# A decode step of a hybrid RG-LRU and mLSTM layer: decode products in pieces of four tokens, and a unit's half products in another order

## The chip, the cores and the metric

The kernel runs on one core of a Trainium2 chip. The metric is the device time of one execution in microseconds, the median of several runs. TensorE (PE) multiplies, VectorE (DVE), ScalarE (ACT) and GpSimd (POOL) work on tiles in SBUF, SyncE (SP) issues loads. POOL issues most stores. Matmul results stand in banks of PSUM.

## The reference

One layer reads 1024 new prompt positions and one new position each for eight running sequences (decode), with one combined input projection to 7168 columns and some gates:

```python
hn = rmsnorm(x, g_norm)
u = hn @ w_in                       # x: 1024 wide; columns xa, za, q, k, v, o, zb, gates
yA, hA, bufA = rglru_branch(xa, ...)
h, C, n, m = mlstm_seq(q, k, v, ig, lf, C0, n0, m0)
yB = sigmoid(uo) * h ; yB = yB * rsqrt(mean(yB * yB) + EPS) * g_mhead
x = x + concat([yA * silu(za), yB * silu(zb)]) @ w_out
```

For a decode token and each of four heads the matrix memory C (256 x 256) is replaced, and its product with the query is wanted:

```python
C_new = carry_scale * C + decay * k[:, None] * v[None, :]
num   = P @ v + ginter * (q @ C)
```

All values are float32. Outputs are the projected prompt and decode rows and all new states, C of every sequence and head among them.

## The kernel before, in words

**Units.** The input projection's weights are cut into blocks of 256 columns, and two of them form one of 14 units (`UNITS`, L44), unit 0 in a start stage, units 1 to 13 in the main loop at the end of the program text shown. A unit holds its raw weights in two tiles, raw0 and raw1, for the lower and upper half of the 1024 input rows; each has two parts, one for each column block. Its product with the prompt is done with seven block products in place of eight: P1, P2, P5, P6, P7, P3, P4 in this order, each in two halves s = 0 and 1. P1, P6, P7 and P4 add into banks X (tag `kv`, one for each half), P2, P5 and P3 into banks Y (tag `o`).

**Splitting.** Each factor is split in a high and a low part, and one logical matmul is three (`mm3`, L66 to L68: high by high, high by low, low by high). A half product is 12 matmuls of 512 columns, or 24 of 256 in units of v and o. `prep` (L276) makes the weights' two parts: ACT casts the high part (L72), DVE subtracts for the low part (L73), into two of six `ws` slots. It runs two products ahead. Before some of them DVE adds or subtracts blocks of raw weights in place (L279 to L288). When P7 or P4 is prepared, the next unit's raw0 or raw1 is loaded whole (L243, two loads of 512 KB on SP's queue).

**Decode rows.** At the preparation of P5, before the raw weights are changed in place, `dec_unit` (L251) multiplies the eight decode rows by the unit's 512 columns: 32 float32 matmuls in four column tiles of 32 (L257), 64 records in the trace.

**Decode states.** When q, k and v of a head are complete, `decode_steps` puts nine steps in a queue: one to set up, and eight tokens. A token's C (two blocks of 128 x 256) is scaled by ACT (L988), gets its outer product from DVE in two instructions (L990), and is stored by POOL. C has four buffers and the broadcast v two. After each second token `products` multiplies the two new states by their queries (L1009): four float32 matmuls in four column tiles, eight records, into bank `qp`.

**What sets the order.** After each half product `pop_bg` takes steps from queues of other work; a token step is taken at every second half, from unit 10 on at every third (`DEC`, L46). `late` holds what follows one or two halves later. When the queues are empty and all heads are complete, `m_start` begins the prompt's matrix part. A scheduler then sets the final order of instructions on each engine by its own estimates, and adds the waits.

Of the kernel before, what the change touches and what calls it, by code (L numbers as in the profile page):

```python
# [9 lines left out]
F32 = mybir.dt.float32  # L10
# [7 lines left out]
P = 128  # L18
# [33 lines left out]
def hymba_kernel(  # L52
# [181 lines left out]
    def load_raw(u, b, parts=(0, 1)):  # L234

        if u >= len(units):
            return
        if (u, b) not in raws:
            raws[u, b] = rawp.tile([P, 4, 512], F32, tag=f"raw{b}", name=f"raw{b}_{u}")
        for a in parts:  # L240
            kind, j = units[u][a]
            c = COL[kind] + j * 256
            ld(raws[u, b][:, :, a * 256:(a + 1) * 256],  # L243
               w_in[0, b * HT:(b + 1) * HT, c:c + 256].rearrange("(k p) c -> p k c", p=P))
# [3 lines left out]
               "z": lambda j: dz[:, 2 * j:2 * j + 2], "x": lambda j: dxz[:, 0, 2 * j:2 * j + 2],  # L248
               "y": lambda j: dxz[:, 1, 2 * j:2 * j + 2]}

    def dec_unit(u):  # L251

        pz = ps("tr" if u < 2 else "o", [P, 512])[:, 0:P]
        for k in range(KC):
            for g in range(4):
                w = blk(u, g // 2, k // 4)[:, k % 4, (g % 2) * P:(g % 2 + 1) * P]
                TE.matmul(pz[32 * g:32 * g + 32, :], hnd[:, NB * k:NB * k + 32], w, start=k == 0, stop=k == KC - 1,  # L257
                          skip_group_check=True)
# [12 lines left out]
    wops = {}  # L271

    def blk(u, a, b):
        return raws[u, b][:, :, a * 256:(a + 1) * 256]

    def prep(u, q):  # L276
        if q == Q_P5:
            dec_unit(u)
            V.tensor_tensor(blk(u, 0, 0), blk(u, 0, 0), blk(u, 1, 0), op=ALU.subtract)  # L279
            V.tensor_tensor(blk(u, 1, 0), blk(u, 1, 0), blk(u, 1, 1), op=ALU.add)  # L280
        if q == Q_P6:
            V.tensor_tensor(blk(u, 1, 0), blk(u, 1, 1), blk(u, 0, 0), op=ALU.subtract)
        src = {Q_P1: (0, 0), Q_P2: (0, 1), Q_P5: (1, 0), Q_P6: (1, 0), Q_P7: (0, 0), Q_P3: (0, 1), Q_P4: (1, 1)}
        hi, lo = ws([P, 4, 256], f"wh{u}_{q}"), ws([P, 4, 256], f"wl{u}_{q}")
        split(hi, lo, blk(u, *src[q]))
        wops[u, q] = hi, lo
        if q == Q_P6:
            V.tensor_tensor(blk(u, 0, 1), blk(u, 0, 1), blk(u, 1, 0), op=ALU.subtract)  # L288
        b = {Q_P7: 0, Q_P4: 1}.get(q)
        if b is not None:  # L290
            if u + 1 < len(units):
                load_raw(u + 1, b)
            else:
                if b == 1:
                    r_open(0)

    px = {}

    def product(u, q):

        kind = units[u][0][0]
        wh, wl = wops.pop((u, q))
        bh, bl = cb[q]
        first, last = q in (Q_P1, Q_P2, Q_P5), q in (Q_P2, Q_P3, Q_P4)
        for s in range(2):
            if q == Q_P1:
                px["X", s] = ps("kv", [P, 512])
            if q in (Q_P2, Q_P5):
                px["Y", s] = ps("o", [P, 512])
            X, Y = px["X", s], px.get(("Y", s))  # L310
            out = X if q in (Q_P1, Q_P6, Q_P7, Q_P4) else Y
            if kind in "vo":
                for i in range(2):
                    t = slice((2 * s + i) * P, (2 * s + i + 1) * P)
                    for k in range(4):
                        mm3(out[:, i * 256:(i + 1) * 256], bh[:, k, t], bl[:, k, t], wh[:, k, :], wl[:, k, :],
                            first and i == 0 and k == 0, last and i == 1 and k == 3)
            else:
                c = slice(s * P, (s + 1) * P)
                for k in range(4):  # L320
                    mm3(out, wh[:, k, c], wl[:, k, c], bh[:, k, :], bl[:, k, :], first and k == 0, last and k == 3)
            evac(u, q, s, X, Y)
            yield

    def evac(u, q, s, X, Y):
        if q == Q_P1:
            px["s1", s] = t = sg([P, 512], "s1")
            A.copy(t, X)
        elif q == Q_P2:
            t = px.pop(("s1", s))  # L330
            V.tensor_tensor(t, t, Y, op=ALU.add)
            emit_out(u, 0, 0, s, t)
        elif q == Q_P5:
            px["s5", s] = t = sg([P, 512], "s5")
            A.copy(t, Y)
# [609 lines left out]

    def dec_open():
        p2 = fpr["p"]
        fetch_C(0)
        fetch_C(1)

        fpr["qsel"] = qsel = p2.tile([P, 2, 36], F32, tag="qsel", name="qsel")
        G.memset(qsel, 0.0)
# [16 lines left out]
    def decode_steps(h):  # L969
# [5 lines left out]
        def first():  # L975
# [5 lines left out]
            fetch_v(h, 0)  # L981

        def token(b):
            i = h * NB + b

            def f():
                vb_, C = ds_.pop(("v", i)), ds_["C", i]
                A.mul(C, C, dGI[:, b, h:h + 1])  # L988
                for kb in range(2):
                    V.scalar_tensor_tensor(C[:, kb, :], vb_, st["kw"][:, kb, b:b + 1], C[:, kb, :],  # L990
                                           op0=ALU.mult, op1=ALU.add)
                stq(s_C[0, b, h].rearrange("(kb p) v -> p kb v", p=P), C)
                if b + 1 < NB:
                    fetch_v(h, b + 1)
                if b % 2:
                    late.append(lambda: late.append(products))
                else:
                    fetch_C(i + 2)
                    fetch_C(i + 3)


            def products():
                if b == 1:
                    st["pq"] = ps("qp", [P, 512])
                pq = st["pq"]
                for g in range(4):
                    bb, kb = b - 1 + g // 2, g % 2
                    q, n = (qfirst[:, kb, bb, :], 32) if b == 1 else (qsel[:, kb, 4 * bb:4 * bb + 4], 4)
                    TE.matmul(pq[32 * g:32 * g + n, 0:256], q, ds_["C", h * NB + bb][:, kb, :], start=b == 1,  # L1009
                              stop=b == NB - 1, skip_group_check=True)  # L1010
                for bb in (b - 1, b):
# [12 lines left out]
        return [first] + [token(b) for b in range(NB)]  # L1024


    def bh(t):
# [645 lines left out]

    gg = gates()
    bg.extend([lambda: next(gg, None)] * 17 + [rd_open])
    last_u = len(units) - 1
    unit_of = {p: u for u, pair in enumerate(units) for p in pair}
    done_h = [max(unit_of[k, h] for k in "qkv") for h in range(NH)]

    def m_start():  # L1680
        state["m"] = True
        bg.append(m_open1)
        for n in range(NH):
            bg.extend(m_first(n))

    preps(LEAD)
    part = 0
    for n, (u, q) in enumerate(seq):
        preps(n + 1 + LEAD)
        for _ in product(u, q):  # L1690
            pop_bg(2 if u == 1 or u == last_u else 1, 1, part % DEC[1 if u >= DEC[0] else 2] == 1)
            part += 1
        if u == last_u:
            wo_due(q)
        if q == 6:
            for kind, j in units[u]:
                if kind == "x":
                    rg_unit(j)
            for half in range(2):
                if u == max(unit_of["v", 2 * half], unit_of["v", 2 * half + 1], 1):  # L1700
                    bg.append(lambda half=half: dec_rows(half))
            for h in range(NH):
                if done_h[h] == u:
                    bg.append(lambda h=h: dcq.extend(decode_steps(h)))
            if u == last_u - 1:
                dgen = decode_outputs()

                def step():
                    next(dgen, None)
                    run_late()  # L1710
                state["out"] = [step] * 5 + [m_open2]
        if not state["m"] and u > max(done_h) and not (bg or rgq or dcq or late):
            m_start()
        if u == last_u and q == 0:
            if not state["m"]:
                while bg or rgq or dcq or late:
                    pop_bg()
                m_start()
            bg.extend(state["out"])
    while bg or late:  # L1720
        pop_bg()
    with tc.issue_after(lastt[0].ins):
# [102 lines left out]
```

## Time and profile before

| | |
|---|---|
| median of 3 runs | 915.67 us (915.23 to 915.72) |
| profiled execution | 913.23 us |
| its span, first to last instruction | 911.3 us |
| PE busy | 899.6 us, 99% |
| DVE, ACT, POOL busy | 739.3, 585.0, 194.2 us |
| mean granted TensorE clock | 0.999 |
| DMA packets | 167.76 MB, mean 184 GB/s |
| split of weights, ACT cast L72 and DVE L73 | 91 each, 1049 ns and 1221 ns |

A row of the timeline has the start in us, the duration in us, the engine, the line, the operation, the target and sources by tile name, the form, and the count; in brackets the idle time before it and what ended it. Matmuls are pipelined, so the durations of neighbours overlap: what one costs is the time from its start to the next start. A float32 matmul leaves two records. A row of the waits has the total, the count and the longest.

### The profile page before, as it was taken

Reading aid. Unit: us, or ns where it says so; the run is one execution under the profiler, and the core shown is the slowest. Engines: PE = TensorE matmul, PEld = TensorE weight load, DVE = VectorE, ACT = ScalarE, POOL = GpSimd, SP = SyncE. Lnnn points to the kernel's source line nnn. Section 1 sums busy time; section 2 is a strip of 40 time slices with the busy share of each in tenths; the row PEclk is TensorE's granted clock in tenths of the full one; section 3 lists DMA queues with packets and bytes.
Section 4 is the critical chain, followed back from the end, with each engine's and each line's share of the span. In section 5 each row is a group of like instructions: output and inputs, shape, how many; then the busy total and the mean of one; then the engine's idle time right before and its main releaser. Section 6 shows DMA issues by size and latency. Waiting matters only on the chain. (4 is left out here: it accounts for less than half of the span.)

```text
span 911.3 us, 16738 instructions
## 1 busy us (share of the span) xinstructions
PE 899.6 (99%) x5889; PEld 762.3 (84%) x5889; DVE 739.3 (81%) x1528; ACT 585.0 (64%) x1086; POOL 194.2 (21%) x322
## 2 busy tenths in 40 slices
PE   8999999999999999999999999999999999999996
PEld 6997778877788997887789999887788888888886
DVE  6974778979698978789889876679998879888973
ACT  7653446867567776576658775446786568566642
POOL 1111112122222232324332334010111111121120
PEclk9999999999999999999999999999999999999999
DMA  6412447465746566548665747345679888855531
GB/s 200 149 64 92 139 147 250 135 205 187 236 128 221 171 203 204 197 145 266 201 237 184 253 139 244 108 133 191 215 234 259 202 216 296 217 142 180 181 124 67
DMA packets 130493, 167.76 MB, mean 184 GB/s; under 512 B 17596, under 2 KB 98564, under 8 KB 130402
## 3 DMA queue, kind: packets, MB, share of 16 engines
q1 hardware_dynamic: 108790, 103.68, 37.4%
q0 software_dynamic: 21616, 63.02, 20.9%
q8 instruction: 46, 0.75, 0.3%
q14 instruction: 37, 0.30, 0.1%
q10 hardware_dynamic: 4, 0.00, 0.0%
HBM read 108.00 MB, written 62.92 MB: 188 GB/s over the span
## 5 line engine op out<-in xcount | busy, mean ns | idle before, releaser
L72 ACT CAST wh<-raw 128x1024 fp32r<-128x1024 f32 x91 | 95.4, 1049 | 79.5 <-DVE raw L280 21.0
L73 DVE TENSOR_TENSOR wl<-raw,wh 128x1024 fp32r<-128x1024 f32 x91 | 111.1, 1221 | 29.4 <-ACT wh L72 15.8
L66 PE MATMUL ps_kv<-cb_hi,wh 128*128 128x512 f32 x320 | 127.4, 398 | 0.0
L68 PE MATMUL ps_kv<-cb_hi,wl 128*128 128x512 f32 x320 | 125.5, 392 | 0.0
L67 PE MATMUL ps_kv<-cb_lo,wh 128*128 128x512 f32 x320 | 125.2, 391 | 0.0
L66 PE MATMUL ps_o<-cb_hi,wh 128*128 128x512 f32 x240 | 95.2, 397 | 0.0
L68 PE MATMUL ps_o<-cb_hi,wl 128*128 128x512 f32 x240 | 93.7, 391 | 0.0
L67 PE MATMUL ps_o<-cb_lo,wh 128*128 128x512 f32 x240 | 93.6, 390 | 0.0
L66 PEld LDWEIGHTS ps_kv<-cb_hi,wh 128*128 128x128 f32 x320 | 60.1, 188 | 15.9 <-issue 3.1
L68 PEld LDWEIGHTS ps_kv<-cb_hi,wl 128*128 128x128 f32 x320 | 60.1, 188 | 13.4 <-issue 0.6
L67 PEld LDWEIGHTS ps_kv<-cb_lo,wh 128*128 128x128 f32 x320 | 60.1, 188 | 12.7 <-issue 0.8
L66 PE MATMUL ps_kv<-wh,cb_hi 128*128 128x256 f32 x192 | 55.1, 287 | 0.0
L67 PE MATMUL ps_kv<-wl,cb_hi 128*128 128x256 f32 x192 | 54.4, 283 | 0.0
L68 PE MATMUL ps_kv<-wh,cb_lo 128*128 128x256 f32 x192 | 54.3, 283 | 0.0
L66 PEld LDWEIGHTS ps_o<-cb_hi,wh 128*128 128x128 f32 x240 | 45.1, 188 | 10.4 <-issue 0.8
L68 PEld LDWEIGHTS ps_o<-cb_hi,wl 128*128 128x128 f32 x240 | 45.0, 188 | 9.9
L66 PE MATMUL ps_o<-wo,mh 128*128 128x512 f32 (+1 forms) x136 | 53.0, 390 | 0.0
L67 PEld LDWEIGHTS ps_o<-cb_lo,wh 128*128 128x128 f32 x240 | 45.1, 188 | 8.9
L68 PE MATMUL ps_o<-wo,ml 128*128 128x512 f32 (+1 forms) x136 | 51.6, 380 | 0.0
L67 PE MATMUL ps_o<-wo,mh 128*128 128x512 f32 (+1 forms) x136 | 51.5, 379 | 0.0
L66 PE MATMUL ps_o<-wh,cb_hi 128*128 128x256 f32 x144 | 41.0, 284 | 0.0
L67 PE MATMUL ps_o<-wl,cb_hi 128*128 128x256 f32 x144 | 40.7, 283 | 0.0
(559 smaller groups left out, 2603.8 us busy)
## 6 DMA issues: line engine op xcount, KB each, us to landing
raw<-in_w_in_dram SPq DMA_DIRECT2D x55, 512.0 KB
Cb<-in_state_mlstm_C_dram SPq DMA_DIRECT2D x32, 256.0 KB
out_dram<-Cb POOLq DMA_DIRECT2D x32, 256.0 KB, 4.9
qk<-d_qk SPq DMA_DIRECT2D x32, 256.0 KB
ring<-d_ro SPq DMA_DIRECT2D x26, 256.0 KB
d_qk<-s POOLq DMA_DIRECT2D x24, 256.0 KB, 4.8
d_x<-s POOLq DMA_DIRECT2D x16, 256.0 KB, 2.8
zsr<-d_y SPq DMA_DIRECT2D x16, 256.0 KB
```

The lines of the kernel that those rows point to most:

```text
L66: TE.matmul(out, ah, bh, start=first, stop=False, skip_group_check=True)
L67: TE.matmul(out, ah, bl, start=False, stop=False, skip_group_check=True)
L68: TE.matmul(out, al, bh, start=False, stop=last, skip_group_check=True)
L72: a = A.copy(hi, src)
L73: V.tensor_tensor(lo, src, hi.bitcast(F32), op=ALU.subtract)
```

## The change

**Decode products.** They are now done for four tokens at a time: eight pieces of eight matmuls (16 records) in place of 16 of four. A piece is put in the queue `full`, and `dec_unit` takes it directly behind its own matmuls. C is fetched four tokens at a time after the products of the four before. The scale by ACT is done one token ahead, and v is fetched two ahead. Tokens are taken at halves 3, 5, 7, 9 and 11 of a unit's 14.

**Half products.** A unit now runs P2s0 P2s1 P1s0 P1s1 P5s0 P5s1 P6s0 P6s1 P3s0 P7s0 P7s1 P3s1 P4s0 P4s1 (the last unit begins with P1). P2's result is copied and P1's added to it, where before P1's was copied. Weights are prepared at halves 0, 2, 4, 6, 8, 11 and 12.

**Raw weights.** raw0 and raw1 are one tile each for all units, and the next unit's weights are loaded by parts as a block is done with: raw0's second part after P6 is prepared, its first after P7, raw1's first after P3, its second after P4. `m_start` is tested after each second half, and its first steps stand some 40 instructions of PE later in unit 12.

```diff
-DEC = 10, 2, 3
+DEC = 3, 5, 7, 9, 11
...
         if (u, b) not in raws:
-            raws[u, b] = rawp.tile([P, 4, 512], F32, tag=f"raw{b}", name=f"raw{b}_{u}")
+            raws[u, b] = raws[0, b] if (0, b) in raws else rawp.tile([P, 4, 512], F32, tag=f"raw{b}", name=f"raw{b}")
...
+        if full:
+            full.popleft()()
         Z = sg([P, P], "Z")
         A.copy(Z, pz)
...
+    FREED = {Q_P6: (0, (1,)), Q_P7: (0, (0,)), Q_P3: (1, (0,)), Q_P4: (1, (1,))}
...
-        b = {Q_P7: 0, Q_P4: 1}.get(q)
-        if b is not None:
-            if u + 1 < len(units):
-                load_raw(u + 1, b)
-            else:
-                if b == 1:
-                    r_open(0)
+        if u + 1 < len(units):
+            if q in FREED:
+                load_raw(u + 1, *FREED[q])
+        elif q == Q_P4:
+            r_open(0)
...
+        if q in (Q_P1, Q_P2):
+            Z = X if q == Q_P1 else Y
+            if ("s1", s) not in px:
+                px["s1", s] = t = sg([P, 512], "s1")
+                A.copy(t, Z)
             else:
+                t = px.pop(("s1", s))
+                V.tensor_tensor(t, t, Z, op=ALU.add)
+                emit_out(u, 0, 0, s, t)
...
+        def ready(b):
+            fetch_v(h, b)
+            fetch_v(h, b + 1)
+            scale(b)
...
-                A.mul(C, C, dGI[:, b, h:h + 1])
+                if b % 4 < 3:
+                    scale(b + 1)
...
-                if b % 2:
-                    late.append(lambda: late.append(products))
-                else:
-                    fetch_C(i + 2)
-                    fetch_C(i + 3)
+                if b % 4 < 2:
+                    late.append(lambda: fetch_v(h, b + 2))
+                if b % 4 == 3:
+                    full.append(products)
...
+                for b0 in (b - 3, b - 1):
+                    for g in range(4):
+                        bb, kb = b0 + g // 2, g % 2
+                        q, n = (qfirst[:, kb, bb, :], 32) if b0 == 0 else (qsel[:, kb, 4 * bb:4 * bb + 4], 4)
+                        TE.matmul(pq[32 * g:32 * g + n, 0:256], q, ds_["C", h * NB + bb][:, kb, :], start=b0 == 0,
+                                  stop=b0 == NB - 2, skip_group_check=True)
...
+                for n in (1, 3):
+                    late.append(lambda n=n: late.append(lambda: [fetch_C(i + n), fetch_C(i + n + 1)]))
...
+        return [first, *steps[:4], lambda: ready(4), *steps[4:]]
...
-    seq = [(u, q) for u in range(1, len(units)) for q in range(7)]
+    last_u = len(units) - 1
+    FIRST = lambda u: (Q_P1, Q_P2) if u == last_u else (Q_P2, Q_P1)
+    seq = [(u, q) for u in range(1, len(units)) for q in (*FIRST(u), *range(2, 7))]
...
+    REST = [(Q_P5, 0), (Q_P5, 1), (Q_P6, 0), (Q_P6, 1), (Q_P3, 0), (Q_P7, 0), (Q_P7, 1), (Q_P3, 1), (Q_P4, 0), (Q_P4, 1)]
+    PREP = 0, 2, 4, 6, 8, 11, 12
...
+    for u in range(1, len(units)):
+        for n, (q, s) in enumerate([(q, s) for q in FIRST(u) for s in range(2)] + REST):
+            if n in PREP:
+                preps(7 * (u - 1) + PREP.index(n) + 1 + LEAD)
+            product(u, q, s)
+            pop_bg(2 if u == 1 or u == last_u else 1, 1, part % 14 in DEC)
```

In the orders below, names end in a running number; `wh4_3` and `wl4_3` are the high and low weights of unit 4's product number 3 (numbers 0 to 6 are P1, P2, P5, P6, P7, P3, P4), `cb_hi` and `cb_lo` the prompt's parts, `hnd` the decode rows, `Cb` a token's C.

PE before, a decode product between the two halves of P6 in unit 4 (L1009):

```order
L67 MATMUL ps_kv_2341<-cb_lo3_194,wh4_3_2400 128x512
L68 MATMUL ps_kv_2341<-cb_hi3_193,wl4_3_2401 128x512
L1009 MATMUL ps_qp_2160<-Cb_2197,qsel_1416 4x256 x2
L1009 MATMUL ps_qp_2160<-Cb_2199,qsel_1416 4x256 x2
L66 MATMUL ps_kv_2367<-cb_hi3_193,wh4_3_2400 128x512
L67 MATMUL ps_kv_2367<-cb_lo3_194,wh4_3_2400 128x512
```

PE now, the decode rows of unit 5 and the second piece of the first head behind them (L1019 is the new line of the products, L259 that of the decode rows):

```order
L259 MATMUL ps_o_2697<-raw0_0_219,hnd_112 32x128 x16
L259 MATMUL ps_o_2697<-raw1_232,hnd_112 32x128 x16
L1019 MATMUL ps_qp_2314<-Cb_2368,qsel_1413 4x256 x2
L1019 MATMUL ps_qp_2314<-Cb_2370,qsel_1413 4x256 x2
L1019 MATMUL ps_qp_2314<-Cb_2372,qsel_1413 4x256 x2
L1019 MATMUL ps_qp_2314<-Cb_2374,qsel_1413 4x256 x2
L66 MATMUL ps_o_2748<-cb_hi1_189,wh5_1_2620 128x512
```

Sixteen groups by themselves became eight groups of twice the size, with decode rows ahead of them.

PE before, from the start stage's end into unit 1 (`ps_tr` takes the decode rows of units 0 and 1, raw1_0 is unit 0's tile, raw0_1 and raw1_1 are unit 1's):

```order
L577 MATMUL ps_o_1017<-wg_213,hnd_112 32x8 x8
L257 MATMUL ps_tr_1029<-raw1_0_232,hnd_112 32x128 x8
L66 MATMUL ps_kv_1123<-cb_hi0_187,wh1_0_1074 128x512
L67 MATMUL ps_kv_1123<-cb_lo0_188,wh1_0_1074 128x512
L257 MATMUL ps_tr_1082<-raw0_1_1064,hnd_112 32x128 x16
L68 MATMUL ps_kv_1123<-cb_hi0_187,wl1_0_1075 128x512
```

PE now, the same place:

```order
L580 MATMUL ps_o_1017<-wg_213,hnd_112 32x8 x8
L259 MATMUL ps_tr_1029<-raw1_232,hnd_112 32x128 x14
L259 MATMUL ps_tr_1080<-raw0_0_219,hnd_112 32x128 x16
L259 MATMUL ps_tr_1080<-raw1_232,hnd_112 32x128 x2
L66 MATMUL ps_o_1121<-cb_hi1_189,wh1_1_1072 128x512
L67 MATMUL ps_o_1121<-cb_lo1_190,wh1_1_1072 128x512
L66 MATMUL ps_o_1174<-cb_hi1_189,wh1_1_1072 128x512
L259 MATMUL ps_tr_1080<-raw1_232,hnd_112 32x128 x14
L68 MATMUL ps_o_1121<-cb_hi1_189,wl1_1_1073 128x512
```

P1's matmuls (wh1_0) stood behind unit 0's decode rows; now P2's (wh1_1) stand there, behind two matmuls on unit 1's raw1, and the six matmuls of unit 0's decode rows that stood in two places of the start stage have come to its end.

PE before, P6 and P7 in unit 1 (L616 transposes parameters):

```order
L67 MATMUL ps_kv_1176<-cb_lo3_194,wh1_3_1230 128x512
L68 MATMUL ps_kv_1176<-cb_hi3_193,wl1_3_1231 128x512
L616 MATMUL ps_s_1166<-idF_78,par_1146 128x49 x8
L66 MATMUL ps_kv_1123<-cb_hi4_195,wh1_4_1275 128x512
L67 MATMUL ps_kv_1123<-cb_lo4_196,wh1_4_1275 128x512
```

PE now:

```order
L67 MATMUL ps_kv_1259<-cb_lo3_194,wh1_3_1228 128x512
L619 MATMUL ps_s_1164<-idF_78,par_1144 128x49 x8
L68 MATMUL ps_kv_1259<-cb_hi3_193,wl1_3_1229 128x512
L66 MATMUL ps_o_1279<-cb_hi5_197,wh1_5_1332 128x512
L67 MATMUL ps_o_1279<-cb_lo5_198,wh1_5_1332 128x512
L66 MATMUL ps_kv_1234<-cb_hi4_195,wh1_4_1274 128x512
L67 MATMUL ps_kv_1234<-cb_lo4_196,wh1_4_1274 128x512
L68 MATMUL ps_o_1279<-cb_hi5_197,wl1_5_1333 128x512
```

P3 (wh1_5) follows P6 (wh1_3) at once, with two matmuls of P7 (wh1_4) ahead of the first use of P3's low part.

More of the change, by code (lines that the diff above doesn't have):

```diff
@@ L249, in hymba_kernel @@
                "y": lambda j: dxz[:, 1, 2 * j:2 * j + 2]}
+    full = deque()
     def dec_unit(u):
@@ L301, in product @@
         kind = units[u][0][0]
-        wh, wl = wops.pop((u, q))
+        wh, wl = wops.pop((u, q)) if s == 1 else wops[u, q]
         bh, bl = cb[q]
         first, last = q in (Q_P1, Q_P2, Q_P5), q in (Q_P2, Q_P3, Q_P4)
[L305 to L317, printed above, removed]
-            else:
[L319 to L332, printed above, removed]
+        if q == Q_P1:
+            px["X", s] = ps("kv", [P, 512])
+        if q in (Q_P2, Q_P5):
+            px["Y", s] = ps("o", [P, 512])
+        X, Y = px.get(("X", s)), px.get(("Y", s))
+        out = X if q in (Q_P1, Q_P6, Q_P7, Q_P4) else Y
@@ new lines, in product @@
+        if kind in "vo":
+            for i in range(2):
+                t = slice((2 * s + i) * P, (2 * s + i + 1) * P)
+                for k in range(4):
+                    mm3(out[:, i * 256:(i + 1) * 256], bh[:, k, t], bl[:, k, t], wh[:, k, :], wl[:, k, :],
+                        first and i == 0 and k == 0, last and i == 1 and k == 3)
+        else:
+            c = slice(s * P, (s + 1) * P)
+            for k in range(4):
+                mm3(out, wh[:, k, c], wl[:, k, c], bh[:, k, :], bl[:, k, :], first and k == 0, last and k == 3)
@@ L947, in dec_open @@
         p2 = fpr["p"]
-        fetch_C(0)
-        fetch_C(1)
+        for i in range(4):
+            fetch_C(i)
         fpr["qsel"] = qsel = p2.tile([P, 2, 36], F32, tag="qsel", name="qsel")
@@ L980, in first, with scale @@
             V.tensor_copy(qfirst[:, :, :, 0], dq[:, 2 * h:2 * h + 2, 0:2])
-            fetch_v(h, 0)
+            ready(0)
+        def scale(b):
+            C = ds_["C", h * NB + b]
+            A.mul(C, C, dGI[:, b, h:h + 1])
+        def ready(b):
+            fetch_v(h, b)
+            fetch_v(h, b + 1)
+            scale(b)
         def token(b):
@@ L992, in f @@
                 stq(s_C[0, b, h].rearrange("(kb p) v -> p kb v", p=P), C)
-                if b + 1 < NB:
-                    fetch_v(h, b + 1)
-                if b % 2:
-                    late.append(lambda: late.append(products))
-                else:
-                    fetch_C(i + 2)
-                    fetch_C(i + 3)
+                if b % 4 < 2:
+                    late.append(lambda: fetch_v(h, b + 2))
+                if b % 4 == 3:
+                    full.append(products)
             def products():
-                if b == 1:
+                if b == 3:
                     st["pq"] = ps("qp", [P, 512])
                 pq = st["pq"]
[L1006 to L1011, printed above, removed]
+                for b0 in (b - 3, b - 1):
[4 more added lines that the diff above has]
+                                  stop=b0 == NB - 2, skip_group_check=True)
+                for bb in range(b - 3, b + 1):
                     del ds_["C", h * NB + bb]
+                for n in (1, 3):
+                    late.append(lambda n=n: late.append(lambda: [fetch_C(i + n), fetch_C(i + n + 1)]))
                 if b == NB - 1:
@@ L1023, in token @@
             return f
-        return [first] + [token(b) for b in range(NB)]
+        steps = [token(b) for b in range(NB)]
+        return [first, *steps[:4], lambda: ready(4), *steps[4:]]
     def bh(t):
@@ L1675, in hymba_kernel @@
     bg.extend([lambda: next(gg, None)] * 17 + [rd_open])
-    last_u = len(units) - 1
     unit_of = {p: u for u, pair in enumerate(units) for p in pair}
@@ L1684, in m_start @@
             bg.extend(m_first(n))
+    REST = [(Q_P5, 0), (Q_P5, 1), (Q_P6, 0), (Q_P6, 1), (Q_P3, 0), (Q_P7, 0), (Q_P7, 1), (Q_P3, 1), (Q_P4, 0), (Q_P4, 1)]
+    PREP = 0, 2, 4, 6, 8, 11, 12
+    DUE = 1, 3, 5, 7, 10, 12, 13
     preps(LEAD)
     part = 0
[L1688 to L1691, printed above, removed]
-            part += 1
[L1693 to L1717, printed above, removed]
-                m_start()
-            bg.extend(state["out"])
@@ new lines, in hymba_kernel, with step @@
+    for u in range(1, len(units)):
[4 more added lines that the diff above has]
+            pop_bg(2 if u == 1 or u == last_u else 1, 1, part % 14 in DEC)
+            part += 1
+            if u == last_u and n in DUE:
+                wo_due(DUE.index(n))
+            if n == 13:
+                for kind, j in units[u]:
+                    if kind == "x":
+                        rg_unit(j)
+                for half in range(2):
+                    if u == max(unit_of["v", 2 * half], unit_of["v", 2 * half + 1], 1):
+                        bg.append(lambda half=half: dec_rows(half))
+                for h in range(NH):
+                    if done_h[h] == u:
+                        bg.append(lambda h=h: dcq.extend(decode_steps(h)))
+                if u == last_u - 1:
+                    dgen = decode_outputs()
+                    def step():
+                        next(dgen, None)
+                        run_late()
+                    state["out"] = [step] * 5 + [m_open2]
+            if n % 2 and not state["m"] and u > max(done_h) and not (bg or rgq or dcq or late):
+                m_start()
+            if u == last_u and n == 1:
+                if not state["m"]:
+                    while bg or rgq or dcq or late:
+                        pop_bg()
+                    m_start()
+                bg.extend(state["out"])
```

4 lines of the change are left out of this document (3 added, 1 removed).

## The prediction

> **What bounds the kernel now.** I read the page's head, then the view of TensorE's waits, then the timeline.
>
> ```profile
> span 911.3 us, 16738 instructions
> PE 899.6 (99%) x5889; PEld 762.3 (84%) x5889; DVE 739.3 (81%) x1528; ACT 585.0 (64%) x1086; POOL 194.2 (21%) x322
> PE ps_tr L531 <- POOL ones L116: 1.1, 1, 1.1
> PE ps_o L67 <- DVE w1l L73: 0.9, 1, 0.9
> PE ps_tr L257 <- DMA raw<-in_w_in_dram: 0.3, 1, 0.3
> ```
>
> TensorE (PE) is busy 899.6 of 911.3 us. The longest single wait is 1.1 us, and no listed wait of a unit's product is for a PSUM bank. So another order of half products can free nothing that the profile shows: I put the spacing of banks at zero. What can change is the time that PE spends in matmuls that do little, and new idle time. The profiled execution took 913.2 us, 2.4 under the median of 915.67; I work on it and carry the difference over.
>
> **Decode products: 16 groups become 8, each behind a unit's decode rows.** The group records at L1009 and one group among 512-column matmuls:
>
> ```profile
> L1009 PE MATMUL ps_qp<-Cb,qsel x96: 379/379/380, 207.6 to 536.4; 128*4 128x256 f32 x96
> L1009 PE MATMUL ps_qp<-Cb,qfirst x32: 379/391/403, 187.3 to 496.1; 128*32 128x256 f32 x32
> 187.01 0.39 PE L68 MATMUL ps_kv<-cb_hi,wl 128*128 128x512 f32 x1
> 187.33 0.64 PE L1009 MATMUL ps_qp<-Cb,qfirst 128*32 128x256 f32 x8
> 188.24 0.39 PE L67 MATMUL ps_kv<-cb_lo,wh 128*128 128x512 f32 x1
> 207.24 0.39 PE L68 MATMUL ps_kv<-cb_hi,wl 128*128 128x512 f32 x1
> 207.56 0.61 PE L1009 MATMUL ps_qp<-Cb,qsel 128*4 128x256 f32 x8
> 208.10 0.50 PE L66 MATMUL ps_kv<-cb_hi,wh 128*128 128x512 f32 x1
> 208.44 0.39 PE L67 MATMUL ps_kv<-cb_lo,wh 128*128 128x512 f32 x1
> 208.67 0.40 PE L68 MATMUL ps_kv<-cb_hi,wl 128*128 128x512 f32 x1
> ```
>
> 128 records in eights are 16 groups. Full-width matmuls start 0.23 us apart (208.44 to 208.67). From 207.24 to 208.44 are 1.20 us, where two steps would take 0.46: the group costs 0.74. At 187 it is 1.23 - 0.46 = 0.77. Four of the one and twelve of the other are 12.0 us. Of this the step from the last full matmul to the group (0.32 for 0.23), and the first full step behind it (0.34 for 0.23), are paid for coming and going, 0.20 a group; the group's own 0.54 holds two rounds of four column tiles.
>
> Now each of eight pieces has four rounds and comes directly behind the 64 records of a unit's decode rows, which pay for coming and going already. How much is a round?
>
> ```profile
> 73.12 1.08 PE L257 MATMUL ps_tr<-raw,hnd 128*32 128x128 f32 x32
> 74.13 0.50 PE L68 MATMUL ps_kv<-cb_hi,wl 128*128 128x512 f32 x1
> 159.12 1.95 PE L257 MATMUL ps_o<-raw,hnd 128*32 128x128 f32 x64
> 161.00 0.50 PE L66 MATMUL ps_kv<-cb_hi,wh 128*128 128x512 f32 x1
> ```
>
> Decode rows: 1.01 us for 32 records and 1.88 for 64, so 0.109 per round of four records and 1.01 - 8 x 0.109 = 0.14 for draining. If a product group drains for as long, its round is (0.54 - 0.14) / 2 = 0.20, and four are 0.80; with the qfirst piece, 0.57 long, 0.83. I take 0.82, so 8 x 0.82 = 6.5. The bounds: were all of a group's 0.54 rounds, a piece costs 1.08 and the saving is 12.0 - 8.6 = 3.4; were coming and going hidden in it as at 0.23 us, a round is 0.155 and the saving 12.0 - 5.0 = 7.0. **Saving 5.5 us.** C is fetched right after a piece, four tokens at a time, and a piece waits on PE only if one of its four states is late; the next unit's decode rows come 14 halves of 12 matmuls at 0.23 us later, 39 us, for eight tokens at the most, so I price that at 0 and keep 0 to 2 us.
>
> By the Trainium skill, "TensorEngine Tiling (Array Packing)", Key Properties, a change of the tiling mode drains TensorE, a change of the tile alone does not. The rows above agree: a group pays for coming and going, a round inside it does not. If the step from the decode rows to the products counted as a change of mode too, each piece would pay one more drain, 0.14 by the row above, and the saving would be 4.4.
>
> **Unit 1 begins with P2, whose weights are not there.** P2 reads block raw1, P1 reads raw0. Unit 1's raw1 can be loaded only when the decode rows of unit 0 have read the old raw1.
>
> ```profile
> 59.24 0.42 PE L257 MATMUL ps_tr<-raw,hnd 128*32 128x128 f32 x6
> 59.59 0.39 PE L66 MATMUL ps_o<-wph,cb_hi 128*128 128x264 f32 x1
> 59.81 0.28 PE L67 MATMUL ps_o<-wpl,cb_hi 128*128 128x264 f32 x1
> 72.45 0.50 PE L66 MATMUL ps_kv<-cb_hi,wh 128*128 128x512 f32 x1
> 72.68 0.98 SPq L243 DMA_DIRECT2D raw<-in_w_in_dram  x2
> 76.74 1.05 ACT L72 CAST wh<-raw 128x1024 fp32r<-128x1024 f32 x1 [3.86 <-DMA raw<-in_w_in_dram]
> 76.76 0.41 PE L257 MATMUL ps_tr<-raw,hnd 128*32 128x128 f32 x4 [0.29 <-DMA raw<-in_w_in_dram]
> 77.82 1.23 DVE L73 TENSOR_TENSOR wl<-raw,wh 128x1024 fp32r<-128x1024 f32 x1 [2.07 <-ACT wh L72]
> 81.64 0.39 PE L66 MATMUL ps_o<-cb_hi,wh 128*128 128x512 f32 x1
> ```
>
> Before, PE goes on with P1 (ps_kv from 72.45) while raw1 travels from 72.68 to 76.74, and P2 starts at 81.64. In the changed order nothing of P1 stands ahead of P2. Reckoned forward: two detours of six records in the start stage (59.24, and one like it) are gone; each cost 0.35, 0.09 coming and 0.10 going, 0.54; their 12 records, three rounds or 0.33, go to the end of unit 0's decode rows. These end at 72.45 - 1.08 + 0.33 = 71.7. The load is issued 0.23 later, 71.9, and lands 4.06 later, 76.0. PE meanwhile has 32 records of unit 1's decode rows on raw0, 1.0 us, and idles from 72.7 to 76.0. Then four records, and idle again until the cast of P2's high half, 1.05, at 77.05. Three full matmuls (0.69) and the other 28 records (seven rounds and the drain, 0.9, and 0.2 coming and going) end at 78.85; the low half is there by 77.1 + 1.23 = 78.4. The remaining 21 matmuls of P2 at 0.23 and two transposes among them (0.1 each, as a round) end at 83.9. There the second product starts; before it was 81.64. **Loss 2.2 us**, the detours' gain in it. The two halves of raw1 are issued together and share the queues; P2 needs one. If it came in half of the 4.06, the loss would be 0.2; if the transfer took a quarter longer, 3.2. What waits there behind ACT's cast is only P1's cast, with 6 us to spare.
>
> **P3 follows P6 at once.** P3's low half needs a ws slot, freed when P5 is done; before, two products (P6, P7) lay between, now one.
>
> ```profile
> 92.31 0.39 PE L68 MATMUL ps_o<-cb_hi,wl 128*128 128x512 f32 x1
> 93.22 1.05 ACT L72 CAST wh<-raw 128x1024 fp32r<-128x1024 f32 x1
> 98.00 1.22 DVE L73 TENSOR_TENSOR wl<-raw,wh 128x1024 fp32r<-128x1024 f32 x1 [4.20 <-PE ps_kv L67]
> 311.82 0.28 PE L68 MATMUL ps_o<-wh,cb_lo 128*128 128x256 f32 x1
> 315.86 1.22 DVE L73 TENSOR_TENSOR wl<-raw,wh 128x1024 fp32r<-128x1024 f32 x1
> ```
>
> From P5's last matmul to the end of P3's low half: 6.9 us in unit 1 (92.31 to 99.22), 5.3 in unit 6 (311.82 to 317.08). The cover is P6's 24 matmuls, 24 x 0.23 = 5.5. Unit 6 fits. In unit 1 the slot is freed by P6 itself (4.20 of waiting for ps_kv L67, since the parameters par hold one), and the changed order puts eight transposes and two matmuls of P7 ahead of the first use; 1.2 + 0.6 us of cover against 1.22 of work. Before, DVE and ACT had no hurry there. I take 0.3 us in all, with 0 and 6 (0.5 in twelve units) as ends.
>
> **The start of the prompt's matrix part**, moved some 40 instructions later in unit 12 and packed closer, reuses ps_qp and ps_s soon after their copies:
>
> ```profile
> 571.98 0.42 DVE L1229 COPY Cf<-ps_qp 128x258 f32<-128x258 f32 x1
> 572.32 0.42 DVE L1229 COPY Cf<-ps_s 128x258 f32<-128x258 f32 x1
> ```
>
> Two such copies less what lies between are about 0.3 us; 0 if DVE is free, 1.5 if each comes behind a 1.22 us split. The loads of raw weights by halves, one scale ahead on ACT, and P2 copied in P1's place keep the number of their instructions and have no wait of PE on them: 0.
>
> **The sum:** -5.5 + 2.2 + 0.3 + 0.3 = -2.7 us: 910.5 for the profiled execution, 913.0 for the median.
>
> **Rivals.** *No hole*: the load is early enough or P1's matmuls run ahead, and the whole saving stays: 915.7 - 5.5 - 0.75 + 0.6 = 910.0. For it: P1's weights have long been in SBUF. Against: the order is fixed and has P2 first. *P3 late in each unit* (the slower side): the low half comes over 5.5 us after P5, because DVE takes other work first; half of unit 1's excess of 1.4, 0.7 us, in each of 12 units is +8.4 in place of 0.3, so 921.1. It decides from 0.4 us a unit: then 913.0 + 4.5 = 917.5. For it: 6.9 and 5.3 us above; against: DVE is idle 19% and knows its order. *The clock falls in the hole.* At the start of the trace PE ran at half pace:
>
> ```profile
> 11.40 0.42 PE L67 MATMUL ps_o<-wpl,b12h 128*128 128x264 f32 x1
> 11.62 0.33 PE L68 MATMUL ps_o<-wph,b12l 128*128 128x264 f32 x1
> 11.79 0.28 PE L66 MATMUL ps_o<-wph,b12h 128*128 128x264 f32 x1
> 11.91 0.29 PE L67 MATMUL ps_o<-wpl,b12h 128*128 128x264 f32 x1
> ```
>
> Steps of 0.22 there become 0.12. Were PE as slow after the hole for as long as the hole lasted, 3.3 us, half of that is lost: +1.7, 914.7. Against it: no wait of PE in the view is over 1.1 us, so the trace does not show that a hole does this. The Trainium skill, "TensorE: Matmul & The Clock Gate", Part 1, has half rate after an idle window of about 3.4 us and full rate after a busy one as long; by it the same 1.7 us would go if a window fell wholly into the hole, and no run so far can show it. *Smaller saving*: C or v late for a piece, or a piece at 1.08: 915.
>
> **How the numbers follow.** The forecast 0.45, no hole 0.14, P3 late 0.16, the clock 0.12, smaller saving 0.13. A measurement here tells 0.2% from no change, 1.8 us: under 913.8 is faster, over 917.5 slower. The forecast's own range is 911.2 to 915.0, two thirds of it faster: 0.30, with no hole 0.14 and a few of the others 0.06, 0.50. Slower is P3 late, 0.16. Same is the rest, 0.34. The range, 909.8 to 918.5, leaves out half of P3 late and the edges of the others.
>
> **What would show it.** L1019 in 8 groups of 16 right behind L259, each adding 0.8 us to 1.88: the first step; 1.1 would be the lower saving. PE's waits with one on raw's DMA of about 3.3 us near 73 to 76, one on ACT wh of 0.7, and the second product at 83.9: the second. PE's waits for DVE wl L73 at ps_o of 0.3 us in all: the third; 5 us there makes me wrong. Full-width steps of 0.46 behind 77 would be the clock. Bank waits that vanish can show nothing, as none is listed; a gain beyond 5.5 us would need another source.

## The result, and the profile after

The changed kernel took 920.71 us in the median of six executions (917.29 to 924.22), against 915.69 before (915.01 to 916.05): a ratio of 1.0058, 95% interval 1.0035 to 1.0081. It is slower by 0.6%, the forecast was 913.0, and 920.71 lies outside the range. Its executions also lie 7 us apart where those of the kernel before lie 1 us apart. The profiled execution is the fastest of them, 917.29 us, 4.1 over the one profiled before.

The page's head, and the waits of TensorE, of the changed kernel:

```profile
span 915.2 us, 16742 instructions
PE 897.3 (98%) x5889; PEld 766.6 (84%) x5889; DVE 739.8 (81%) x1528; ACT 586.0 (64%) x1086; POOL 194.9 (21%) x322
```

```profile
PE ps_o L67 <- DVE wl L73: 3.1, 2, 1.9
PE ps_tr L259 <- DMA raw<-in_w_in_dram: 2.5, 1, 2.5
PE ps_s L1311 <- DVE kl L1214: 0.6, 1, 0.6
PE ps_o L66 <- ACT wh L72: 0.4, 1, 0.4
```

PE is busy 2.3 us less, and the span is 3.9 us longer: there are new waits, one for unit 1's raw1 and two for a low half of weights. The start of unit 1 in the timeline, and the same stretch in windows of 2 us (a window's row has its length first, then PE's busy time, and behind the five engines' busy times the granted clock):

```profile
72.17 1.08 PE L259 MATMUL ps_tr<-raw,hnd 128*32 128x128 f32 x32 [0.36 <-ACT Z L264]
75.70 0.64 PE L259 MATMUL ps_tr<-raw,hnd 128*32 128x128 f32 x4 [2.46 <-DMA raw<-in_w_in_dram]
76.78 0.80 PE L66 MATMUL ps_o<-cb_hi,wh 128*128 128x512 f32 x1 [0.44 <-ACT wh L72]
80.80 0.63 PE L66 MATMUL ps_o<-cb_hi,wh 128*128 128x512 f32 x1
81.23 0.63 PE L67 MATMUL ps_o<-cb_lo,wh 128*128 128x512 f32 x1
82.25 0.39 PE L67 MATMUL ps_o<-cb_lo,wh 128*128 128x512 f32 x1
82.48 0.39 PE L68 MATMUL ps_o<-cb_hi,wl 128*128 128x512 f32 x1
86.15 0.39 PE L66 MATMUL ps_kv<-cb_hi,wh 128*128 128x512 f32 x1
```

```profile
72.00:74.00 2.00, 1.08 (x32) 0.81 (x32) 0.00 (x0) 0.11 (x1) 0.00 (x0) 1.00 0.73 171
74.00:76.00 2.00, 0.30 (x4) 0.18 (x4) 0.00 (x0) 0.32 (x1) 0.00 (x0) 0.77 1.06 359
76.00:78.00 2.00, 1.56 (x7) 0.83 (x3) 1.25 (x2) 1.67 (x2) 0.00 (x0) 0.50 0.25 76
78.00:80.00 2.00, 2.00 (x29) 1.36 (x28) 2.00 (x3) 0.00 (x0) 0.00 (x0) 0.50 0.04 8
80.00:82.00 2.00, 2.00 (x8) 1.49 (x5) 1.66 (x2) 0.27 (x1) 0.00 (x0) 0.52 0.00 0
82.00:84.00 2.00, 2.00 (x11) 1.60 (x10) 0.26 (x2) 0.41 (x1) 0.00 (x0) 1.00 0.00 0
```

PE waits 2.46 us for the load and 0.44 for the cast, in the places that the prediction named; it had 3.3 and 0.7. Then full-width matmuls start 0.43 us apart (80.80 to 81.23), not 0.23 as from 82.25 on: the clock granted falls to half at about 75.1, during the wait (2 us at 0.77 are 0.9 us of half clock, the last of the window), and stays there until 82. The second product starts at 86.15; before, it was at 81.64.

The two waits for wl are P3's, in units 6 and 10, whose products are of 256 columns. In unit 10, from SyncE's, VectorE's, ScalarE's and PE's rows:

```profile
474.18 2.00 SPq L970 DMA_DIRECT2D Cb<-in_state_mlstm_C_dram  x4
486.65 0.37 SPq L243 DMA_DIRECT2D raw<-in_w_in_dram  x1
487.11 1.66 SPq L964 DMA_DIRECT2D vbc<-d_dv  x2
490.72 0.49 DVE L1003 SCALAR_TENSOR_TENSOR Cb<-vbc,kw,Cb 128x256 f32<-128x256 f32 x1 [2.23 <-DMA vbc<-d_dv]
491.84 0.63 ACT L381 ACTIVATE s<-s 128x512 f32<-128x512 f32 x1 [1.38 <-DVE s L334]
496.26 1.05 ACT L72 CAST wh<-raw 128x1024 fp32r<-128x1024 f32 x1
498.71 1.22 DVE L73 TENSOR_TENSOR wl<-raw,wh 128x1024 fp32r<-128x1024 f32 x1
499.99 0.39 PE L67 MATMUL ps_o<-wl,cb_hi 128*128 128x256 f32 x1 [1.16 <-DVE wl L73]
```

SyncE has nothing issued from 476.2 to 486.65, when a load of raw weights has its wait behind it; only then come the requests for v. VectorE stands 2.23 us for v, with the evacuation of another sum (L334) behind it, ScalarE stands 1.38 us for that, and its cast for P3 comes later for it: from 491.84 to the cast at 496.26 ScalarE has no gap.

In unit 6 VectorE stands for v too, 1.05 us at 307.0, but the wait that it has directly ahead of P3's low half is for another small load, xs:

```profile
321.21 0.17 DVE L811 COPY OC<-xs 128x3 f32<-128x3 f32 x1 [1.39 <-DMA xs<-d_x]
322.57 0.39 PE L67 MATMUL ps_o<-wl,cb_hi 128*128 128x256 f32 x1 [1.92 <-DVE wl L73]
```

So this trace shows the whole chain from v to PE in unit 10 alone. VectorE's waits for v in the two kernels, before first:

```profile
DVE Cb L990 <- DMA vbc<-d_dv: 3.6, 3, 3.2
```

```profile
DVE Cb L1003 <- DMA vbc<-d_dv: 17.8, 12, 2.7
```

The products themselves, a piece behind decode rows in unit 5:

```profile
250.34 1.95 PE L259 MATMUL ps_o<-raw,hnd 128*32 128x128 f32 x64
252.11 1.05 PE L1019 MATMUL ps_qp<-Cb,qsel 128*4 128x256 f32 x16
253.08 0.50 PE L66 MATMUL ps_o<-cb_hi,wh 128*128 128x512 f32 x1
```

From 250.34 to 253.08 are 2.74 us, 0.86 more than the 1.88 of decode rows alone.

### The profile page after: what moved, and what is told of

Same layout as the page of the kernel before. It is cut to its first block, busy times and chain, and to the rows that moved or that the text cites. A ratio compares the mean times of both kernels' runs of the same rounds, so it can differ in the third digit from the quotient of the medians.

```text
span 915.2 us, 16742 instructions
## 1 busy us (share of the span) xinstructions
PE 897.3 (98%) x5889; PEld 766.6 (84%) x5889; DVE 739.8 (81%) x1528; ACT 586.0 (64%) x1086; POOL 194.9 (21%) x322
## 5 line engine op out<-in xcount | busy, mean ns | idle before, releaser
L1003 DVE SCALAR_TENSOR_TENSOR Cb<-vbc,kw,Cb 128x256 f32<-128x256 f32 x64 | 28.4, 480 | 19.7 <-DMA vbc<-d_dv 17.8
```

## The experiments

**Undo one thing at a time.** Theory A: idle PE in unit 1, with the half clock behind it, makes most of the loss. Rivals B and C: the loss comes from the order of halves in all units, or is P3's place.

`e1_p1_first` lets unit 1 begin with P1 again:

```diff
-    FIRST = lambda u: (Q_P1, Q_P2) if u == last_u else (Q_P2, Q_P1)
+    FIRST = lambda u: (Q_P1, Q_P2) if u in (1, last_u) else (Q_P2, Q_P1)
```

> The changed kernel with one thing undone: unit 1 begins with P1 again, as the last unit does, so that its first product needs no weights that are still on their way. Theory A (idle TensorE at the start of unit 1, and the half clock behind it, make most of the loss and all of the spread between executions): the 4.6 us by which unit 2 began late go, granted clock back at 0.999, about 913 us, executions within 1.5 us of each other. Theory B (the loss is spread over the units, by the new order of halves): 919 us or more and the same spread of 5 to 7 us.

Measured: 915.78 us (913.30 to 919.14), ratio 1.0014 (1.0003 to 1.0024). The wait in unit 1 is gone and so are some 4 us, but neither 913 nor the narrow spread came. Its trace has half clock in another place, behind P3's late weights in unit 10:

```profile
493.95 0.39 PE L66 MATMUL ps_o<-wh,cb_hi 128*128 128x256 f32 x1 [0.51 <-ACT wh L72]
496.59 0.39 PE L67 MATMUL ps_o<-wl,cb_hi 128*128 128x256 f32 x1 [2.25 <-DVE wl L73]
```

```profile
496.00:498.00 2.00, 1.41 (x8) 1.41 (x9) 1.94 (x5) 1.98 (x3) 0.00 (x0) 0.79 0.57 161
498.00:500.00 2.00, 2.00 (x12) 2.00 (x11) 1.93 (x4) 1.93 (x6) 0.00 (x0) 0.50 0.75 241
500.00:502.00 2.00, 2.00 (x16) 2.00 (x16) 1.93 (x6) 1.95 (x4) 1.40 (x3) 0.86 0.28 47
```

`e2_warm` puts 14 matmuls that nothing reads into the wait of unit 1:

```diff
         for k in range(KC):
+            if u == 1 and k == KC // 2:
+                pw = ps("qp", [P, 512])
+                for i in range(14):
+                    TE.matmul(pw, cb[Q_P1][0][:, 0, 0:P], cb[Q_P1][0][:, 0, :], start=True, stop=True)
             for g in range(4):
```

> The changed kernel with 14 matmuls of 512 columns added into an unused bank while TensorE waits for unit 1's weights; they work on the prompt's P1 operand and nothing reads the result. The wait stays, TensorE is not idle in it. If idleness lowers the clock (theory A): steps of 0.23 us behind the wait in place of 0.43, second product at 83.8 us in place of 86.15, some 2.4 us or more less in the median (917 to 918) and executions closer together. If the clock falls for another cause (the load, or the switch of tile forms): steps of 0.43 and 86 us as before, 920.7 us, perhaps 0.2 more for the added work.

Measured: 922.27 us (921.31 to 923.98), ratio 1.0083. In the trace the second product starts at 84.0 us with the clock at 1.00 throughout, as expected; the time did not follow. PE waited 4.1 us for wl and 2.3 for wh in units 6 and 10, longer than in the changed kernel, and had half clock after both. The time of this run decides nothing on unit 1; it is repeated below without those waits.

`e3_p7_before_p3`, and `e4_both` with the edit of e1 as well:

```diff
-    REST = [(Q_P5, 0), (Q_P5, 1), (Q_P6, 0), (Q_P6, 1), (Q_P3, 0), (Q_P7, 0), (Q_P7, 1), (Q_P3, 1), (Q_P4, 0), (Q_P4, 1)]
-    PREP = 0, 2, 4, 6, 8, 11, 12
-    DUE = 1, 3, 5, 7, 10, 12, 13
+    REST = [(Q_P5, 0), (Q_P5, 1), (Q_P6, 0), (Q_P6, 1), (Q_P7, 0), (Q_P7, 1), (Q_P3, 0), (Q_P3, 1), (Q_P4, 0), (Q_P4, 1)]
+    PREP = 0, 2, 4, 6, 8, 10, 12
+    DUE = 1, 3, 5, 7, 9, 11, 13
```

> The changed kernel with P7 put back between P6 and P3 (halves P5 P5 P6 P6 P7 P7 P3 P3 P4 P4, weights prepared at every second half). Theory A: the two waits for P3's low half in units 6 and 10, 3.1 us in the profiled execution, go, about 917.3 us; the spread of executions stays, since the hole in unit 1 stays. Rival C (these waits only move to P7 or P4, or are not what differs): 920 us or more.

> Both: unit 1 with P1 first, and P7 before P3. What is left of the change is the decode products in pieces of four, P2 ahead of P1 in units 2 to 12, and the loads by parts. Theory A: the saving of the products alone is left, 5.0 us from the traces, less some 0.7 us that I have not placed: 911 us, executions within 1.5 us. Theory B or a saving that is not there: 915 us or more.

Measured: 919.27 us (917.97 to 922.24), ratio 1.0051, and 914.40 us (912.01 to 918.60), ratio 0.9997 (0.9984 to 1.0010). Both expectations of A failed: P3's waits went and a longer one came. P7 adds into the bank that P6 has left, so it waits until ScalarE has copied P6's sum (L341), and ScalarE is late in the same places. PE's waits of e3, its row in unit 10, and the windows behind it, with the clock again at half:

```profile
PE ps_kv L66 <- ACT s L341: 6.5, 3, 4.9
```

```profile
502.54 0.58 PE L66 MATMUL ps_kv<-wh,cb_hi 128*128 128x256 f32 x1 [4.86 <-ACT s L341]
```

```profile
500.00:502.00 2.00, 0.00 (x0) 0.00 (x0) 2.00 (x3) 1.97 (x4) 0.00 (x0) 0.62 0.61 203
502.00:504.00 2.00, 1.46 (x7) 1.46 (x8) 1.90 (x6) 1.97 (x4) 0.00 (x0) 0.50 0.31 44
504.00:506.00 2.00, 2.00 (x11) 2.00 (x11) 1.97 (x4) 1.91 (x6) 0.00 (x0) 0.50 0.63 218
506.00:508.00 2.00, 2.00 (x14) 2.00 (x14) 1.93 (x5) 1.70 (x3) 1.79 (x3) 0.68 0.42 125
```

So P3's place is not the cause by itself; it chooses which late work of ScalarE or VectorE PE meets. What makes those engines late?

**v earlier.** Theory D: v makes VectorE late, VectorE ScalarE, and both PE. Rival E: units 6 and 10 simply hold too much work for them. `e5_v_ahead` gives v four buffers in place of two and asks for it four tokens ahead:

```diff
-        ds_["v", h * NB + b] = t = fpr["p"].tile([P, 256], F32, tag="vbc", name="vbc", bufs=2)
+        ds_["v", h * NB + b] = t = fpr["p"].tile([P, 256], F32, tag="vbc", name="vbc", bufs=4)
...
         def ready(b):
-            fetch_v(h, b)
-            fetch_v(h, b + 1)
+            if b == 0:
+                for i in range(4):
+                    fetch_v(h, i)
...
-                if b % 4 < 2:
-                    late.append(lambda: fetch_v(h, b + 2))
+                if b < 4:
+                    late.append(lambda: fetch_v(h, b + 4))
```

> The changed kernel with four buffers for v in place of two, and v requested four tokens ahead. In the changed kernel VectorE waits 17.8 us for v (12 times), because the loads of v stand in SyncE's queue behind loads of raw weights by halves that wait themselves. Theory D (late v holds VectorE, then ScalarE, and so the weights' high half of P3 in units 6 and 10): VectorE's wait for v under 6 us, TensorE's waits for wl in units 6 and 10 gone, 3 us and in some executions a half clock less: 916.5 to 918.5, the hole of unit 1 being left. Rival E (the waits in units 6 and 10 come from ACT and DVE having too much work there, whatever v does): waits and time as before, 920 to 921.

Measured: 912.80 us (912.39 to 913.85), ratio 0.9983 (0.9974 to 0.9992): 0.75% of the time less than the changed kernel, some 7 us, by this edit alone, and a spread of 1.5 us. That is more than D had expected. Of the profile: VectorE's wait for v is 4.1 us, no wait of a unit's product for wl is left, and the only wait of PE over 1.2 us is the one in unit 1. The edit changes the number of buffers and the place of the requests together, and with them the scheduler's order (the copy L811 no longer stands directly ahead of unit 6's P3 low half), so which of these does it is not shown.

```profile
PE ps_tr L259 <- DMA raw<-in_w_in_dram: 2.5, 1, 2.5
```

`e6_p1_first_v` has the edits of e1 and e5, `e7_both_v` those of e4 and e5.

> Unit 1 with P1 first, and v four tokens ahead; P3 still directly behind P6. Theory A with D: neither the hole nor late weights, granted clock 0.999 in all executions, 910.5 to 912 us and a spread under 1.5 us. Rival E: 915.8 us as with P1 first alone.

> As the run before, and P7 between P6 and P3 as well. Theory D: what TensorE waited for there (8.7 us on ScalarE's copy of P6's sum, before P7 adds into the same bank) goes too, 910.5 to 912 us. If the spacing of banks matters by itself, the copy is late here and not in the run before: 912 to 914 us with waits on ScalarE's copy in units 6, 9 or 10.

Measured: e6 908.63 us (908.46 to 909.83), ratio 0.9936 (0.9924 to 0.9949), the fastest kernel of this study, below the 910.5 to 912 that D had expected. e7 911.26 us (909.35 to 912.21), ratio 0.9962 (0.9949 to 0.9974). With v in time, P7 behind P6 still meets ScalarE's copy, and P3 between them does not:

```profile
PE ps_kv L66 <- ACT s L341: 1.8, 3, 0.9
```

So the place of P3 is worth 2.6 us here (e7 against e6), and this row, a wait for a bank, has 1.8 of them.

The four kernels with and without the edits of e1 and e5 agree with each other: P1 first in unit 1 takes off 0.44% without v ahead (the changed kernel to e1) and 0.47% with it (e5 to e6), and v ahead takes off 0.75% with P2 first (the changed kernel to e5) and 0.78% with P1 first (e1 to e6).

**The decode part alone.** `e8_products_alone` takes the order of halves, the tiles and the whole loads of raw weights back to those of the kernel before (the lists REST, PREP and DUE, not shown again, are those of e3); `e10_products_v` adds the edit of e5; `e9_before_v` is the kernel before with v four tokens ahead and nothing else.

```diff
-            raws[u, b] = raws[0, b] if (0, b) in raws else rawp.tile([P, 4, 512], F32, tag=f"raw{b}", name=f"raw{b}")
+            raws[u, b] = rawp.tile([P, 4, 512], F32, tag=f"raw{b}", name=f"raw{b}_{u}")
...
-    FREED = {Q_P6: (0, (1,)), Q_P7: (0, (0,)), Q_P3: (1, (0,)), Q_P4: (1, (1,))}
+    FREED = {Q_P7: (0, (0, 1)), Q_P4: (1, (0, 1))}
...
-    FIRST = lambda u: (Q_P1, Q_P2) if u == last_u else (Q_P2, Q_P1)
+    FIRST = lambda u: (Q_P1, Q_P2)
```

> The kernel before with the decode part of the change alone: products by four tokens behind the decode rows, C by fours, tokens at halves 3, 5, 7, 9, 11; the order of halves, the tiles and the loads of raw weights stay whole and as before. The saving of the products by the traces is 5.0 us: 909.5 to 911 us. If v is late without loads by halves too, VectorE waits for it over 10 us, TensorE waits in units 6, 9 or 10, and it is 912 to 915 us.

> The decode part alone, with v four tokens ahead. Theory D: the waits of 4.6 us on ScalarE's copy of P6's sum shrink to under 2 us and the saving of the products, 5.0 us, shows: 910 to 911.5 us. If it stays at 914 the products' saving is lost elsewhere, and the order of halves is what gains.

> The kernel before with four buffers for v and v requested four tokens ahead, nothing else. VectorE waited 3.6 us for v there (3 times) and TensorE for no bank. Theory D: nothing to gain, 914.6 us like the kernel before, within 0.5 us; so that the 6 us between the kernel before and P1 first with v ahead are the change's own. Rival: earlier v speeds the kernel before as well, 912 us or less, and then the gain is v's.

Measured: e8 914.65 us (913.20 to 916.26), ratio 1.0000 (0.9992 to 1.0009); e10 913.75 us (911.34 to 916.16), 0.9989 (0.9978 to 1.0000); e9 914.43 us, 0.9999 (0.9990 to 1.0008). v ahead gives the kernel before nothing. In e8 VectorE waits 19.3 us for v, and PE 4.6 us for ScalarE's copy, although the raw weights are loaded whole, so v is late without the loads by halves too: the decode part is enough. And in e10, with 0.3 us of waiting for v, PE still waits 2.5 us for ScalarE's copy and 1.0 for VectorE's evacuation, both in order to write into a bank:

```profile
PE ps_kv L66 <- ACT s L341: 2.5, 2, 2.1
PE ps_o L66 <- DVE s L334: 1.0, 2, 0.6
```

The expectation for e10 failed: 0.9 us are left of a saving of 5.0, and these two waits for banks, which the kernel before did not have, are 3.5 of the 4.1 that are missing. The order of halves of before does not carry the new rhythm of tokens; e6 does. Of the 5.1 us between e10 and e6, P3's place has the 2.6 of e7 against e6; how the rest falls on P2 ahead of P1 and on the loads by parts was not taken apart.

**The changed kernel again, and the clock.** `a2_changed_again` has no edit, `e12_warm_v` is e5 with the unread matmuls of e2.

> The changed kernel unaltered, for a second trace and its spread. Theory A with D: TensorE's wait in unit 1 and half clock behind it as before, waits for wl in units 6 and 10 of another length than 1.9 and 1.2 us, and where one is over some 2 us a second stretch of half clock near 500 us; 917 to 924 us. Rival: the executions differ in another place.

> The changed kernel with v four tokens ahead, and the 14 unread matmuls in the wait of unit 1 again. The first try of these matmuls was overlaid by the waits in units 6 and 10, which v ahead takes away. If idle time lowers the clock: no half clock at 76 to 82 us, second product at 84.0 in place of 86.0 us, 910.8 us (912.8 less 2.0). If only the wait itself costs: 912.8 us or 0.2 more.

Measured: a2 921.36 us (917.44 to 924.06), ratio 1.0080. The profiled execution is the fastest again: waits for wl of 3.0 us in units 6 and 10, the longer 2.1, and half clock only from 75.9 to 82.7. The longer executions were not caught in a trace of this kernel; that they have half clock near 500 us too is argued from the traces of e1, e3 and e4, not shown. Their mean granted clock points the same way: 0.994 in the execution of 917.29 us, 0.991 in that of 924.22. But 0.003 of 920 us is 2.8 us, less than half of the 6.9 between the two; where the rest lies is open.

e12: 911.34 us (910.81 to 911.92), ratio 0.9960 (0.9947 to 0.9974), 0.23% or 2.1 us under e5. The clock stays at 1.00 and the second product starts at 83.79; in e5 it is 85.50, in e6 81.40. Two windows of e12, and the row of the second product's start in e12, e5 and e6:

```profile
76.00:78.00 2.00, 1.94 (x32) 1.04 (x32) 1.28 (x2) 1.64 (x2) 0.00 (x0) 1.00 0.24 69
78.00:80.00 2.00, 2.00 (x23) 1.54 (x12) 2.00 (x3) 0.27 (x1) 0.00 (x0) 1.00 0.00 0
```

```profile
83.79 0.40 PE L66 MATMUL ps_kv<-cb_hi,wh 128*128 128x512 f32 x1
```

```profile
85.50 0.39 PE L66 MATMUL ps_kv<-cb_hi,wh 128*128 128x512 f32 x1
```

```profile
81.40 0.39 PE L66 MATMUL ps_o<-cb_hi,wh 128*128 128x512 f32 x1
```

So it is PE's idle time that lowered the clock in unit 1, and matmuls without use prevented it.

## Why the prediction was wrong

**The account of the median**, in ratios to the kernel before: everything in its place (e6) 0.9936; unit 1 with P2 first adds 0.47% (e5), half of it clock (e12); v late adds 0.75%, which makes 1.0058. In microseconds -5.9, +4.3 and +6.9, together +5.3, which is 0.58%; the interval of the changed kernel's ratio leaves the 6.9 uncertain by some 2 us. The forecast had -5.2 for the first (-5.5 and 0.3 for unit 12), +2.2 for the second and +0.3 for the third.

1. *What bounds the kernel.* Right that PE does, wrong in what followed from it. "Another order of half products can free nothing that the profile shows" held for the old rhythm of tokens. The change moves the tokens, ScalarE and VectorE come later to the copies, and the order is then worth 2.6 us (e7 against e6), 1.8 of them waits for a bank. I read the waits of before as if the engines behind them stayed where they were.
2. *The decode products*, -5.5 us: right within 0.4. A piece costs 0.86 us where I took 0.82, so 12.0 - 8 x 0.86 is 5.1; the further drain of 0.14, for 4.4, did not show. Without the new waits (e6) unit 13 starts 5.3 us earlier than in the kernel before. Its first row, before and in e6:

```profile
611.31 0.50 PE L66 MATMUL ps_kv<-cb_hi,wh 128*128 128x512 f32 x1
```

```profile
606.02 0.50 PE L66 MATMUL ps_kv<-cb_hi,wh 128*128 128x512 f32 x1
```

3. *Unit 1*, +2.2 us: the waits are right in kind and place, and the term is mis-sized by the clock. Without half clock the second product starts where I put it: 83.79 in e12, 83.9 in the forecast, 2.2 us behind the 81.64 of before. In the changed kernel's trace it is at 86.15, another 2.4 us later, so that the term measured 4.5 there. I carried the half clock as a rival at 0.12 with 1.7 us, on top of a forecast without it; with a wait reckoned at 3.3 us it belonged into the sum. Of the rule of the Trainium skill ("TensorE: Matmul & The Clock Gate", Part 1) named there, the length of the window is borne out: by the windows' rows (2 us at 0.77 hold 0.9 us of half clock, and so on) the stretches of half clock are 6.8 us long in the changed kernel and 3.4 in e1, two and one of the page's windows of some 3.4 us. That a whole window has to be idle is not: the clock fell at 75.1, 1.8 us behind the end of the last matmul before the wait (72.17 + 1.08).
4. *P3 late*, +0.3 us: the step that failed. I priced it by how late the weights were before, and took VectorE and ScalarE to have time. The waits are 3.1 us in the fastest execution, and late v as a whole, with what half clock comes of it, is by e5 some 7 us in the median. Of the 4.9 us between the two profiled executions of the changed kernel and e5, 3.1 are these waits and 0.7 the later second product of unit 1 (86.15 against 85.50); the rest is not placed. The cause was in another of my lines: "a piece waits on PE only if one of its four states is late", with 0 to 2 us for C or v. I looked for v's lateness at PE. It strikes at VectorE, which stands on it with other work queued behind, 17.8 us in place of 3.6; unit 10 shows this as far as PE, and in unit 6 the load of xs has part of it. The rival "P3 late" has the sign and the place, but neither its reason, other work taken first, since VectorE has the same work between cast and low half in unit 10 of e5, without a wait, nor its spread over all units: unit 1 and ten others had no such wait.
5. *Unit 12*, +0.3 us: no new wait for a bank shows there; 0. The 0.6 us for kl among the waits stands at 676 us, where the kernel before has one of 0.4 (for hh).

The range ended at 918.5 because the rival's price was given a chance of 0.16 and half of it cut off.

## What to carry to other kernels

An engine that takes its work in order, as VectorE does here with L334 behind its wait for v, holds up everything behind one small load, so the slack of a load is to be reckoned at the engine that reads it, and not at the engine that sets the end. A reordered list of products keeps its cost only while the engines that empty the banks keep theirs: price the two together. And where a change leaves TensorE idle for 2 to 3 us, put a stretch of half clock into the sum, or give it something to multiply: against e12, 3.4 us of half clock cost e5 1.7 us by the second product of unit 1 (85.50 against 83.79), and 6.8 cost the changed kernel 2.4 (86.15).

## What the runs showed of the hardware

The clock falls after less idle time than I had thought, and not each time. A wait of 1.9 us in unit 6 of the changed kernel and one of 2.1 us in a2 left it at full. Waits of 0.51 and 2.25 us with a single matmul between them (e1) halved it, as did 2.46 and 0.44 us with four records between (unit 1), and 4.86 us (e3). The half clock begins in the wait or behind it (at 75.1 in a wait until 75.7 in the changed kernel, at 77.8 behind a wait until 75.8 in e5) and lasts 3.4 us (e1; unit 1 of e3 and e5) or 6.8 (unit 1 of the changed kernel; unit 10 of e3). So the same wait costs a varying amount. The ten executions of e5, whose one long wait is that of unit 1, point the same way: six took 912.4 to 912.9 us at a mean granted clock of 0.996, four 913.4 to 913.9 at 0.994.

The column of the granted clock does not show the half pace at the start of the kernel: it has 1.00 from 10 to 12 us in the kernel before, where the rows have steps of 0.22 us that become 0.12.
